# Splitting half of the last store into 112 + 8 + 8 rows, so that eight DMA engines carry 9 row halves and eight carry 7

## Chip, cores, metric

One core of a Trainium2 chip. The metric is the device time of one execution in microseconds; all runs quoted are at full clock. The kernel before took 781.05 us (three runs, 780.86 to 781.10).

## The reference

```python
# logits (32, 128, 4, 4096) f32, prior (32, 128, 4) f32
prior_probs = softmax(prior, axis=-1)
mixture = np.sum(prior_probs[..., None] * softmax(logits, axis=-1), axis=2)   # (32, 128, 4096)
```

For each of 4096 rows, four softmaxes over 4096 columns are mixed with four weights: 268 MB are read and 67 MB written, with little arithmetic for each byte.

## The kernel before

A tile is 128 rows, one on each partition; there are 32 tiles (`U = 32`). ScalarE takes the exponentials with their sums, VectorE weighs and adds, and two sets of buffers alternate. Loads are issued by SyncE and most stores by ScalarE. The very last tile is finished and stored in two column halves, which is what the change touches:

```python
def store(u, acc, eng, lo=0, hi=V):
    st = eng.dma_start(out=ov[u // J, u % J, :, lo:hi], in_=acc[:, lo:hi])
    stores[u] = only(st, adds[u, H - 1])        # waits for the last add alone
# ... (cut)
for k in range(g, h + 1):
    n = 2 if u == U - 1 and k == H - 1 else 1   # last tile, last head: two column halves
    w = V // n
    for c in range(n):
        add(k, mul, c * w, (c + 1) * w)
        if n > 1:
            store(u, acc, nc.sync, c * w, (c + 1) * w)
```

The softmax here doesn't subtract the row's maximum and nothing guards it: scores larger than these inputs give would overflow.

## Time and profile before

| | before |
|---|---|
| time, us (median of the first 3 runs) | 781.05 |
| span of the profiled execution, us | 779.3 |
| busy: VectorE, ScalarE, DMA | 67%, 60%, 99.9% |
| first half of the last store issued, us | 771.19 |
| VectorE done, us | 773.42 |
| last landing, us | 778.37 |
| first half's issue to last landing ("the tail"), us | 7.18 |

The first rows say that the DMA engines are the bound; the others lay out the end, the only place that the change can reach. The timeline of SyncE's issues at the end has two pieces, whose columns are start, duration, engine, line, operation and tiles:

```profile
771.19 0.33 SPq L113 DMA_DIRECT2D out_dram<-ltile  x1
773.45 0.33 SPq L113 DMA_DIRECT2D out_dram<-ltile  x1
```

The reader is to see that the second half is issued 0.03 us after VectorE ends and that nothing more is issued afterwards; the other 5 us are the DMA engines emptying their queues.

### The profile page before, as it was taken

The page shows a single profiled execution, that of the slowest core. Times are in us where ns is not written, and L with a number is a line of the kernel's source. Part 1 is how long each engine was busy: PE and PEld are TensorE (multiplying, and loading weights), DVE is VectorE, ACT ScalarE, POOL GpSimd, SP SyncE. Part 2 cuts the span into 40 slices and gives each one's busy share as a digit, 9 for nine tenths or more (in the row PEclk, how much of TensorE's full clock was granted, in tenths as well). Part 3 has the DMA queues.
Part 4 walks back from the last instruction along what each step waited for, and adds up shares of the span by engine and source line. Part 5 has one row for each costly group of instructions (what it writes and reads, how often), then busy time and mean ns, then how long its engine had stood idle before and what let it go on. Part 6 is the DMA issues. An engine that isn't in the chain of part 4 may idle for free.

```text
span 779.3 us, 654 instructions
## 1 busy us (share of the span) xinstructions
DVE 521.0 (67%) x174; ACT 466.7 (60%) x258; POOL 8.3 (1%) x41
## 2 busy tenths in 40 slices
DVE  4447875558755587555775557855578655689886
ACT  4476555775457755577555675546765567657782
POOL 0000000000000000000000000000000000000000
DMA  9999999999999999999999999999999999999998
GB/s 407 457 417 401 470 407 434 428 461 428 405 467 403 458 420 433 442 443 418 431 454 407 454 408 467 420 415 447 432 442 417 463 399 463 410 427 433 434 429 377
DMA packets 10117, 335.66 MB, mean 431 GB/s; under 512 B 1136, under 2 KB 1136, under 8 KB 1152
## 3 DMA queue, kind: packets, MB, share of 16 engines
q1 hardware_dynamic: 6048, 276.83, 82.3%
q10 hardware_dynamic: 4064, 58.79, 17.6%
q14 instruction: 5, 0.04, 0.0%
HBM read 268.50 MB, written 67.11 MB: 431 GB/s over the span
## 4 chain that ended last, share of the span: by engine, by line
DMA 64%; ACT 27%; DVE 6%; issue 2%; POOL 0%; DVEq 0%; POOLq 0%
DMA ltile<-in_logits_dram 62%; ACT ebuf L159 19%; ACT ltile L159 8%; DVE obuf L177 5%; DMA out_dram<-obuf 2%; DVE ltile L183 1%; POOL coeff L170 0%; DVE rden L168 0%; DVEq L240 0%; POOLq L240 0%; POOLq L170 0%
## 5 line engine op out<-in xcount | busy, mean ns | idle before, releaser
L183 DVE SCALAR_TENSOR_TENSOR obuf<-ebuf,coeff,obuf 128x4096 f32<-128x4096 f32 x90 | 403.6, 4484 | 3.8 <-POOL coeff L170 0.6
L159 ACT ACTIVATE ebuf<-ltile 128x4096 f32<-128x4096 f32 x90 | 322.9, 3589 | 7.4 <-DMA ltile<-in_logits_dram 7.4
L159 ACT ACTIVATE ltile<-ltile 128x4096 f32<-128x4096 f32 x38 | 137.3, 3614 | 280.6 <-DMA ltile<-in_logits_dram 280.6
L168 DVE RECIPROCAL rden<-dsum 128x4 f32<-128x4 f32 (+1 forms) x36 | 6.3, 175 | 227.9 <-ACT ebuf L159 225.1
L177 DVE TENSOR_SCALAR obuf<-ltile,coeff 128x4096 f32<-128x4096 f32 x30 | 70.6, 2353 | 10.2 <-POOL coeff L170 10.2
L183 DVE SCALAR_TENSOR_TENSOR ltile<-ltile,coeff 128x4096 f32<-128x4096 f32 (+1 forms) x7 | 27.0, 3875 | 0.8 <-POOL coeff L170 0.6
L159 ACT ACTIVATION_READ_ACCUMULATOR ebuf<-ltile 128x1 f32 x90 | 16.8, 186 | 0.0
L170 POOL TENSOR_TENSOR coeff<-rden,pp 128x4 f32<-128x4 f32 (+1 forms) x36 | 7.2, 200 | 755.3 <-DVE rden L168 745.4
L159 ACT ACTIVATION_READ_ACCUMULATOR ltile<-ltile 128x1 f32 x38 | 7.1, 186 | 0.0
L139 DVE TENSOR_REDUCE pmax<-pr 16x256 f32<-16x1024 f32 x1 | 1.2, 1208 | 7.8 <-DMA pr<-in_prior_dram 7.8
L141 ACT ACTIVATE pr<-pr 16x1024 f32<-16x1024 f32 x1 | 1.1, 1055 | 7.8 <-DVE pr L140 7.8
L177 DVE TENSOR_SCALAR ltile<-ltile,coeff 128x4096 f32<-128x4096 f32 x2 | 4.7, 2354 | 0.6 <-POOL coeff L170 0.6
L144 DVE TENSOR_TENSOR pn<-pr,pmax 16x1024 f32<-16x1024 f32 x1 | 1.9, 1939 | 0.1
L141 ACT ACT_TABLE_LOAD x1 | 1.3, 1283 | 1.2 <-PEq L229 1.2
L142 DVE TENSOR_REDUCE pmax<-pr 16x256 f32<-16x1024 f32 x1 | 1.2, 1207 | 1.1 <-ACT pr L141 1.1
L149 DVE STREAM_TRANSPOSE pp<-pn 32x256 f32<-32x256 f32 x4 | 1.7, 435 | 0.1
L143 DVE RECIPROCAL pmax<-pmax 16x256 f32<-16x256 f32 x1 | 1.7, 1741 | 0.0
L140 DVE TENSOR_TENSOR pr<-pr,pmax 16x1024 f32<-16x1024 f32 x1 | 1.2, 1211 | 0.0
L138 POOL MEMSET pn<- 32x1024 f32 x1 | 0.9, 941 | 0.3 <-POOLq L229 0.3
L229 POOL MEMSET const-bfloat16-1.0<- 128x1 bf16 x1 | 0.1, 106 | 0.0
L229 POOL MEMSET const-uint8-127<- 128x1 uint8 x1 | 0.1, 106 | 0.0
L229 POOL MEMSET const-float32-0.0<- 128x1 f32 x1 | 0.1, 103 | 0.2 <-issue 0.2
(1 smaller groups left out, 0.1 us busy)
## 6 DMA issues: line engine op xcount, KB each, us to landing
out_dram<-obuf ACTq DMA_DIRECT2D x28, 2048.0 KB, 29.4
ltile<-in_logits_dram SPq DMA_DIRECT2D x7, 4096.0 KB, 26.1
ltile<-in_logits_dram SPq DMA_DIRECT2D x2, 2048.0 KB, 30.9
out_dram<-obuf SPq DMA_DIRECT2D x2, 2048.0 KB, 33.9
out_dram<-ltile SPq DMA_DIRECT2D x1, 2048.0 KB, 17.2
out_dram<-ltile SPq DMA_DIRECT2D x2, 1024.0 KB, 4.8
ltile<-in_logits_dram SPq DMA_DIRECT2D x28, 30.9
pr<-in_prior_dram ACTq DMA_DIRECT2D x1, 64.0 KB, 7.0
```

Of the source, the lines that this page charges most:

```text
L139: nc.vector.reduce_max(pmax, pr, axis=AX.X)
L140: nc.vector.tensor_sub(pr, pr, pmax.unsqueeze(2).to_broadcast([G, R, H]))
L141: nc.scalar.activation(pr, pr, AF.Exp)
L142: nc.vector.reduce_sum(pmax, pr, axis=AX.X)
L143: nc.vector.reciprocal(pmax, pmax)
L144: nc.vector.tensor_mul(pn[0:G].rearrange("g h r -> g r h"), pr, pmax.unsqueeze(2).to_broadcast([G, R, H]))
L149: nc.vector.transpose(pp[32 * t : 32 * (t + 1)], pq[:, :, :, 32 * t : 32 * (t + 1)])
L159: ex = nc.scalar.activation(es[h], lt[:, h], AF.Exp, accum_out=dsum[:, u, h : h + 1])
L168: rc = nc.vector.reciprocal(rden[:, u, h : h + n], dsum[:, u, h : h + n])
L170: mul = nc.gpsimd.tensor_mul(coeff[:, u, h : h + n], rden[:, u, h : h + n], ppu[:, h : h + n])
L177: st = nc.vector.tensor_scalar(out=acc[:, lo:hi], in0=es[h][:, lo:hi], scalar1=coeff[:, u, h : h + 1], scalar2=None, op0=ALU.mult,)
L183: st = nc.vector.scalar_tensor_tensor(out=acc[:, lo:hi], in0=es[h][:, lo:hi], scalar=coeff[:, u, h : h + 1], in1=acc[:, lo:hi], op0=ALU.mu ...
```

## The change

The intent is to level the ragged end: some DMA engines finish later than others, so the first eight engines get 9 row halves in the first half store and the other eight get 7, in place of 8 each.

```diff
-    def store(u, acc, eng, lo=0, hi=V):
-        st = eng.dma_start(out=ov[u // J, u % J, :, lo:hi], in_=acc[:, lo:hi])
-        stores[u] = only(st, adds[u, H - 1])
+    def store(u, acc, eng, lo=0, hi=V, rows=((0, P),)):
+        for a, b in rows:
+            st = eng.dma_start(out=ov[u // J, u % J, a:b, lo:hi], in_=acc[a:b, lo:hi])
+            stores[u] = only(st, adds[u, H - 1])
@@ in the loop over the column halves
-                            store(u, acc, nc.sync, c * w, (c + 1) * w)
+                            rows = ((0, 112), (112, 120), (120, P)) if c == 0 else ((0, P),)
+                            store(u, acc, nc.sync, c * w, (c + 1) * w, rows)
```

## The prediction

> **What bounds the kernel now.** I read the page first, then the chain of waits, then the last few microseconds in short stretches, then the single packet and landing records of the trace. The page:
>
> ```profile
> DVE 521.0 (67%) x174; ACT 466.7 (60%) x258; POOL 8.3 (1%) x41
> ...
> DMA  9999999999999999999999999999999999999998
> ...
> q1 hardware_dynamic: 6048, 276.83, 82.3%
> q10 hardware_dynamic: 4064, 58.79, 17.6%
> q14 instruction: 5, 0.04, 0.0%
> ...
> HBM read 268.50 MB, written 67.11 MB: 431 GB/s over the span
> ```
>
> The reader should see that no compute engine is over 67%, while the 16 DMA engines are busy in every slice: 82.3 + 17.6 = 99.9% of 16 engines' span. The kernel moves 335.6 MB, and that is its time. No byte is removed by the change, so all but the last few microseconds of the 779.3 us span stay as they are. Queue 14 has five small instruction fetches; they matter below.
>
> How does it end? The two half stores of the last tile are the last work. The page's issue line, the waits of the DMA queue of SyncE in the last 16 us, and the stretches of the end:
>
> ```profile
> out_dram<-ltile SPq DMA_DIRECT2D x2, 1024.0 KB, 4.8
> ```
> ```profile
> SPq L113 <- DVE ltile L183: 16.3, 2, 14.4
> SPq L240 <- DMA out_dram<-ltile: 4.4, 2, 2.4
> ```
> ```profile
> 770.00:772.00 2.00, 2.00 (x2) 0.00 (x0) 0.00 (x0) 1.00 0.96 410
> 772.00:774.00 2.00, 1.42 (x1) 0.00 (x0) 0.00 (x0) 1.00 1.00 410
> 774.00:776.00 2.00, 0.00 (x0) 0.00 (x0) 0.00 (x0) 1.00 1.01 422
> 776.00:777.00 1.00, 0.00 (x0) 0.00 (x0) 0.00 (x0) 1.00 0.96 401
> 777.00:777.25 0.25, 0.00 (x0) 0.00 (x0) 0.00 (x0) 1.00 0.33 131
> 777.25:777.50 0.25, 0.00 (x0) 0.00 (x0) 0.00 (x0) 1.00 0.24 98
> 777.50:777.75 0.25, 0.00 (x0) 0.00 (x0) 0.00 (x0) 1.00 0.16 66
> 777.75:778.00 0.25, 0.00 (x0) 0.00 (x0) 0.00 (x0) 1.00 0.00 0
> ```
>
> The last two columns are the DMA share and GB/s; a packet counts where it starts. Up to 777.00 all engines run, although VectorE finished at 773.42 (764.29 + 9.13 in the timeline): the stores stand in line behind earlier traffic. The chain of waits printed in the profile ends at VectorE's drain, but that is the inference losing the DMA; SyncE's final wait ends with the store's landing. After 777.00 comes a ragged end: (0.33 + 0.24 + 0.16) x 0.25 us x 16 = 2.9 us of engine time, nine packets of 0.309 us. Some engines are simply later than others. That raggedness is what the change is aimed at.
>
> The packet records say by how much. Each half store is 128 packets of 8 KB, 8 for each engine, 0.309 us each (26.5 GB/s). The completion packets after the very last one start at 777.05 to 777.16 (ten engines), 777.23, 777.32, 777.48, 777.74, 777.87 and 778.01; the landing follows 0.36 us later (the last at 778.37). The mean is 777.29, so perfect balance would save 778.01 - 777.29 = 0.72 us, 0.09%. That is the ceiling of any change of this kind.
>
> Why three stragglers? The 16 landings of a whole-tile load at 136 us spread over 0.44 us. After the fetch at 147.9 us one landing trails by 0.75 us, after that at 194.0 us another by 1.18; the one at 704.7 us adds a third at 0.64. The late places persist because no engine ever idles to catch up.
>
> **What the Trainium skill says.** "DMA: Bandwidth & Descriptors", section "Why a DMA increments its semaphore by 16 and not by 1": a transfer runs on the largest k up to 16 that divides its slowest dimension, the lowest-numbered k of the core's engines. So 112 rows use 16 engines with 7 rows each, and 8 rows use engines 0 to 7 with one row each. The trace agrees for 16 (the prior load of 16 rows left 16 packets of 4 KB); it has no case of 8 and doesn't number the engines.
>
> "SBUF - State Buffer", section "Door 1: The DMA port swizzle": DMA bandwidth depends on how many of 16 ports the partitions reach; partitions 112 to 115 share one port, likewise 116 to 119, 120 to 123 and 124 to 127. The same DMA page, "The descriptor swizzle", has each engine of a 128-partition transfer on one port of its own. The trace has one sign that crowding costs: the prior load writes 16 rows into partitions 0 to 15, four ports by that table. Its packets take 0.159 us, but the 32 KB packets behind them take 1.55 us on all engines (one 1.67) where others take 1.213: 0.34 us too much. The first store, also a switch of queue, has 2.418 us packets behind it as everywhere, so switching isn't the cost. It could still be that queue's first use.
>
> "Runtime: NRT & Kernel Launch", section "Instruction fetch mechanics": the sequencer fetches its own instructions through its own DMA queue. The trace agrees: the five queue 14 packets of 8 KB, at 147.9, 194.0, 511.1, 704.7 and 774.8 us, and the stragglers of above.
>
> **The change part by part.** Removed: one issue of 128 half rows. Added: one of 112 and two of 8. Bytes, arithmetic and the second half's issue are the same.
>
> *Issue.* The first half is issued at 771.19 for 0.333 us, the second at 773.45, when its VectorE piece ends. Two more issues with their semaphore waits take about 2 x 0.38 = 0.76 us and end near 772.3, before 773.45. First packets come 0.83 us after issue (772.02); the 8-row transfers are ready near 772.4 and 772.8, before the 7 rows are through (772.02 + 7 x 0.31 = 774.2). Cost 0. The second half's first packets are ready near 774.28, so a fast engine with 7 rows may idle under 0.1 us; it isn't last.
>
> *Balance.* If the three stragglers have numbers 8 to 15, each loses one packet: the last completion goes from 778.01 to 777.70. The first eight gain one: from 777.05-777.48 to 777.36-777.79. The end becomes 777.70 to 777.79: -0.22 to -0.31 us. If one of the last two stragglers is in the first eight it ends at 777.87 or 778.01 plus 0.31: +0.17 to +0.31 us.
>
> *Ports.* The last 16 rows are read by engines 0 to 7, four at once from one port. The prior load's excess was 0.34 us for 4 KB rows; estimate for 8 KB: 0.68 us, twice, 1.35 us for the first eight. They have 777.70 - 777.5 = about 0.2 us to spare, so the end would move by about +0.8 to +1.1 us against before. Seven rows for each engine no longer match groups of four partitions either; I allow 0 to 0.5 us for that (estimate: up to a fifth of 7 x 0.309).
>
> *End.* SyncE waits for the semaphores two at a time in fixed order; before, the store's was in the second last pair, with one 0.06 us step behind it. Two more transfers shift the numbering: 0 to +0.06 us.
>
> **Rivals.**
> 1. Balance alone works: about 780.8 us. For it: the stragglers are real and steady, and the first load's engines start as a group of seven at 1.02-1.07 us and nine at 1.16-1.58 us, which looks like a first and a second eight, the second later. Against: fetches, not start order, made the stragglers.
> 2. The stragglers are among the first eight: 781.05 + 0.3 = 781.35. I can't exclude it, for the records carry no engine number; whoever chose the first eight presumably had a reason.
> 3. Port crowding eats the gain: 781.9 to 782.6. For it: the 0.34 us behind the prior load, equal on all engines. Against: that was writing, and a lone case.
> 4. An additional fetch from the longer instruction stream falls on a straggler: +0.3 us. The one at 774.8 fell on an engine that ended at 777.13, so I give it little.
>
> **Range and chances.** I give rival 1 about 0.35, rivals 2 and 4 together 0.2, rival 3 0.45. The middle of that mixture is about 781.3, slightly slower than 781.05 and my choice; 780.6 to 782.6 spans from the full gain with a little noise (the three runs spread 0.24 us) to port crowding in both the small transfers and the seven-row one. 2% is 15.6 us, while all of the last store lasts under 6 us: within 2% is close to sure.
>
> **What would show it.** Queue 1 has more packets: 16 + 8 + 8 completion packets for the first half in place of 16. If 8 KB packets near 774.2-775 stay at 0.31 us, ports don't matter; if the 8-row ones, or those behind them, take 0.6 to 1.2 us, rival 3 holds. If the ragged end narrows and the last landing comes near 778.1, rival 1 holds; if one engine ends near 778.3 with 17 even packets of 0.309 us, rival 2. The prediction is wrong if anything before 771 us moves, or if the small transfers start late enough to hold up the second half.

## The result, and the profile after

The changed kernel took 782.74 us (median of 6, 782.36 to 783.16) against 781.11 (median of 6, 780.86 to 781.13). The ratio is 1.0021, 95% interval 1.0008 to 1.0034. Ratios are the mean time of one kernel's fast runs over that of the other's in the same rounds, so not quite the ratio of the medians. So the change costs 1.6 us, a fifth of a per cent: "same" at 2%, and just above the predicted range (780.6 to 782.6).

In the profile the tail grew from 7.18 to 9.14 us (771.02 to 780.17), by 1.96 us; that it began 0.17 us earlier hides a part. These are the stretches of the end (stretch, its length, three engines, clock, DMA share, GB/s); those of before stand in the prediction:

```profile
770.00:772.00 2.00, 2.00 (x2) 0.00 (x0) 0.00 (x0) 1.00 1.00 418
772.00:774.00 2.00, 1.26 (x1) 0.00 (x0) 0.00 (x0) 1.00 1.00 336
774.00:776.00 2.00, 0.00 (x0) 0.00 (x0) 0.00 (x0) 1.00 0.94 279
776.00:778.00 2.00, 0.00 (x0) 0.00 (x0) 0.00 (x0) 1.00 0.89 348
778.00:780.00 2.00, 0.00 (x0) 0.00 (x0) 0.00 (x0) 1.00 0.18 74
```

This is the line to learn from. Between 772 and 776 the engines are as busy as before (0.94 to 1.00), but they move 336 and 279 GB/s where they moved 410 and 422. Busy here means "a packet is under way", and the packets had become slow. An 8 KB packet took 0.309 us before; in the changed kernel 46 of the 256 took over 0.4 us (3 of 256 before), and the slowest five, starting at 774.6 to 775.0, when the 8-row transfers run, 1.10, 1.17, 1.35, 1.41 and 1.52 us. The time beyond 0.309 us of all these packets together, the excess, is 18.1 us, or 1.13 us for each of 16 engines, against 0.10 before.

The page's queue and issue lines, and SyncE's waits of the last 19 us:

```profile
q1 hardware_dynamic: 6064, 276.83, 82.2%
q10 hardware_dynamic: 4064, 58.79, 17.6%
q14 instruction: 5, 0.04, 0.0%
```
```profile
out_dram<-ltile SPq DMA_DIRECT2D x1, 1024.0 KB, 6.9
out_dram<-ltile SPq DMA_DIRECT2D x1, 896.0 KB, 4.8
```
```profile
SPq L114 <- DVE ltile L184: 15.1, 2, 14.4
SPq L244 <- DMA out_dram<-ltile: 6.0, 1, 6.0
```

The bytes are those of before and the packets 16 more (6064 to 6048): the completion packets of two transfers on eight engines each, as predicted. The second half, issued as early as before (773.29, VectorE had ended at 773.26), needs 6.9 us to land in place of 4.9 (773.45 to 778.37), and SyncE's last wait for it is 6.0 us long.

### The profile page after: what moved, and what is told of

Its sections match the earlier page's. It is cut to its first block, busy times and chain, and to the rows that moved or that the text cites. A ratio compares the mean times of both kernels' runs of the same rounds, so it can differ in the third digit from the quotient of the medians.

```text
span 781.1 us, 656 instructions
## 1 busy us (share of the span) xinstructions
DVE 521.0 (67%) x174; ACT 466.9 (60%) x258; POOL 8.4 (1%) x41
## 3 DMA queue, kind: packets, MB, share of 16 engines
q1 hardware_dynamic: 6064, 276.83, 82.2%
## 4 chain that ended last, share of the span: by engine, by line
DMA 64%; ACT 27%; DVE 6%; issue 2%; POOL 0%; DVEq 0%; POOLq 0%
DMA ltile<-in_logits_dram 62%; ACT ebuf L160 19%; ACT ltile L160 8%; DVE obuf L178 5%; DMA out_dram<-obuf 2%; DVE ltile L184 1%; POOL coeff L171 0%; DVE rden L169 0%; DVEq L244 0%; POOLq L244 0%; POOLq L171 0%
```

## The experiments

The theory after the result: SBUF's side is crowded. Rows 112 to 119 lie on two ports, four on each, by the port table of the Trainium skill ("SBUF - State Buffer", section "Door 1: The DMA port swizzle"), so four engines would read from one port at once; the 112-row transfer may be crowded too. Rivals: small transfers or additional issues cost this much wherever they read; or the stragglers sit among the first eight engines, which were given more.

"Scratch" runs leave the kernel before as it is and add a store from the finished half tile into an internal scratch tensor, so that load is added and nothing taken away. All ten kernels gave the correct result.

On noise: the 95% intervals of these ratios reach 1.0 to 1.3 us to either side (spread rows below: 0.9995 to 1.0022), so a difference under 1 us rests on two other things: whether the ranges of the runs lie apart, and the tail, which comes from one profiled execution of each kernel.

**Issues alone.**

```diff
-   store(u, acc, nc.sync, c * w, (c + 1) * w)
+   cuts = (0, 1792, 1920, 2048) if c == 0 else (2048, 4096)
+   for lo, hi in zip(cuts, cuts[1:]):
+       store(u, acc, nc.sync, lo, hi)
```

> The first half of the last store goes as three transfers of all 128 rows, 1792, 128 and 128 columns wide: the byte split 7:1:1... of the changed kernel, but on all engines and each engine on its own port. Port theory (crowding of rows 112 to 127 on four ports made the loss): 781.1 to 781.4 us, for two more issues cost nothing. Rival (two more issues, completions and small packets in the tail cost the 1.6 us): 782.4 or more.

Measured 781.12 us against 781.00; tail 7.24 us, +0.06. Three issues in place of one, with the same split of bytes (14:1:1 in columns as in rows, not the 7:1:1 of the expectation), cost next to nothing. Additional issues are out; transfers of few rows are tested next.

**Two additional 8-row stores, spread and crowded.** The rows 0, 4, .., 28 lie on eight different ports, the rows 112 to 119 on two.

```diff
+   if c == 0:   # spread: rows 0:32:4 and 1:32:4; crowded: rows 112:120 and 120:128
+       only(nc.sync.dma_start(out=scratch[0:8, 0:2048], in_=acc[0:32:4, 0:2048]), adds[u, k])
+       only(nc.sync.dma_start(out=scratch[8:16, 0:2048], in_=acc[1:32:4, 0:2048]), adds[u, k])
```

> The kernel before, with two additional 8-row half stores (two more 8 KB packets for each of the first eight engines, 0.62 us each) into a scratch tensor, from rows 0,4,..,28 and 1,5,..,29, which lie on eight different ports. Port theory: packets stay near 0.31 us; the end is 781.1 to 781.3 us if the stragglers are engines 8 to 15, and 781.7 if the last one is among the first eight. Rival (8-row transfers are slow by themselves, wherever they read): 782.5 or more.

> The same two additional 8-row half stores into scratch, but read from rows 112 to 119 and 120 to 127, four rows on one port. Port theory: each takes about 1.2 us in place of 0.31 on the first eight engines, 2.4 us in all, so they end near 779.6 to 780 and the time is 782.4 to 783.2 us. Rival (8-row transfers as such, or imbalance): the same time as with the spread rows.

Spread 781.62 us (+0.62 against 781.00), crowded 783.55 (+2.55), with equal bytes and transfers; in the edit only the partitions differ. The ranges lie apart (781.54 to 781.87 and 783.48 to 783.63), and the crowded time is above its expected 782.4 to 783.2. The tails are 7.81 and 9.78 us, so four rows on a port cost 1.97 us for two such transfers. The stretches, first of the spread run, then of the crowded one:

```profile
774.00:776.00 2.00, 0.00 (x0) 0.00 (x0) 0.00 (x0) 1.00 0.88 361
776.00:778.00 2.00, 0.00 (x0) 0.00 (x0) 0.00 (x0) 1.00 0.80 328
```
```profile
774.00:776.00 2.00, 0.00 (x0) 0.00 (x0) 0.00 (x0) 1.00 1.06 266
776.00:778.00 2.00, 0.00 (x0) 0.00 (x0) 0.00 (x0) 1.00 0.75 242
```

In each stretch compare GB/s with the share. Spread: 361 at 0.88, 328 at 0.80, both 410 GB/s for a fully busy set of engines, the usual rate. Crowded: 266 at 1.06 and 242 at 0.75, so 251 and 323. The packets themselves are slow; the slowest took 2.11 us.

The spread run also answers the second rival. Its last completion packets start at 777.31 to 777.40 on eight engines, at 777.85 to 777.90 on five, and at 778.27, 778.34 and 778.62 on three. An engine with two more packets can't be among the early eight: the earliest of before ended at 777.05, and 0.62 us later is 777.67. So the early eight are those without an additional packet. The stragglers of before, at 777.74 or later, aren't among them; so all three are among the eight engines that an 8-row transfer uses, and the last of them ends 0.62 us (two packets) later than before. In that run the second half was also issued late (773.80), which left a doubt: the next pair of runs.

**One additional store, and four-row stores.**

```diff
+   if c == 0:   # once: rows 0:32:4 alone; four rows: 0:16:4 and 1:16:4
+       only(nc.sync.dma_start(out=scratch[0:8, 0:2048], in_=acc[0:32:4, 0:2048]), adds[u, k])
```

> The kernel before with one additional 8-row half store into scratch from rows 0, 4, .., 28 (eight different ports). If the last straggler is one of the first eight engines, one more packet moves the end by 0.31 us: 781.3 to 781.4 us, and two gave 0.62. If the 0.62 us of the run with two came from the later issue of the second half, 781.0 to 781.1 us here, for one more issue ends before that half is ready.

> The kernel before with two additional 4-row half stores into scratch, rows 0, 4, 8, 12 and 1, 5, 9, 13: two more packets for each of the first four engines only. If the last straggler is among engines 0 to 3: 781.6 us, as with the 8-row ones. If among 4 to 7: 781.0 to 781.1 us, and only the second or third straggler or none moves in the landings.

One store: 781.13 us against 781.02, nearer to the second expectation, with overlapping ranges (781.07 to 781.17 and 780.88 to 781.13). The time alone doesn't settle it. The profile speaks for the first: the tail is 7.48 us, +0.30, and it began 0.17 us earlier than in before's profile. A measure that doesn't depend on the start is the time from the last landing of the whole-tile store ahead (the latest engine's) to the last landing of all: before 773.53 to 778.37, 4.84 us; with one additional packet 773.35 to 778.50, 5.15; with two 773.51 to 778.98, 5.47. That is 0.31 us for each packet, with the second half issued on time (773.28) in the run with one. Its packets stay fast too (2 of 264 over 0.4 us), so spread rows don't owe their speed to a late second half. Four-row stores: 781.62 us (+0.60), 773.57 to 779.03, 5.46 us: the latest straggler is even among the four engines that a 4-row transfer uses. If the late engines keep their order, the second latest behaves likewise: from its landing in the store ahead to its last packet it takes 4.49 us before (773.38 to 777.87) and 5.11 in this run (773.39 to 778.51); the third apparently isn't.

**112 rows and one transfer of 16.**

```diff
-   rows = ((0, 112), (112, 120), (120, P)) if c == 0 else ((0, P),)
+   rows = ((0, 112), (112, P)) if c == 0 else ((0, P),)
```

> First half as 112 rows and one transfer of 16 rows on all engines: 8 packets for each engine, no imbalance, and the same four crowded ports. Port theory: 4 rows on a port at a time, about +0.9 us, and something for the 112 rows: 782.0 to 783.2 us. Rival (the loss came from two packets too many on late engines among the first eight): 781.1 us.

Measured 782.17 us against 781.00, tail 8.34 us: +1.17 and +1.16. Every engine should have its 8 packets here, so 1.2 us of loss come without any imbalance. The packets are slow instead, by 1.10 us of excess for each engine, and the rate shows it:

```profile
774.00:776.00 2.00, 0.00 (x0) 0.00 (x0) 0.00 (x0) 1.00 0.97 287
```

**Every other row.**

```diff
-   rows = ((0, 112), (112, 120), (120, P)) if c == 0 else ((0, P),)
+   rows = ((0, 112), (112, P, 2), (113, P, 2)) if c == 0 else ((0, P),)   # used as slices
```

> The changed kernel, but the two 8-row transfers take rows 112, 114, .., 126 and 113, 115, .., 127: two rows on a port at a time instead of four, same bytes, same engines. Port theory: the two transfers lose about 0.3 us each in place of about 0.9, so the time falls from 782.7 to 781.7 to 782.3 us. Rival (the rows 112 to 127 or the 9-to-7 split as such make the loss): 782.7 us still.

Measured 781.75 us against 781.00; the changed kernel had 782.74 against 781.11. Taking two rows from a port instead of four, with the same bytes and rows, cuts the loss from 1.63 to 0.75 us; 0.9 us come back, and the excess falls from 18.1 to 12.0 us, 0.75 us for each of the eight engines. (The profiled executions differ more, tails of 9.14 and 7.70 us.) One thing besides differs: SyncE took 0.78 and 1.37 us to issue the two strided transfers, so the second half went out only at 774.18, 0.86 us after VectorE had ended. That leaves engines idle (12 to 15 packets under way near 775), but it may also thin the traffic beside the small transfers; this run doesn't part the two effects. The stretch of this run beside the changed kernel's 279 GB/s at 0.94:

```profile
774.00:776.00 2.00, 0.00 (x0) 0.00 (x0) 0.00 (x0) 1.00 0.93 340
```

**Two transfers of 64 rows.**

```diff
-   rows = ((0, 112), (112, 120), (120, P)) if c == 0 else ((0, P),)
+   rows = ((0, 64), (64, P)) if c == 0 else ((0, P),)
```

> First half as rows 0 to 63 and rows 64 to 127, both on 16 engines with 4 packets each. Port theory: each reaches only eight ports, two engines on each, so 4 x 2 x 0.309 = 2.47 us a transfer in place of 1.24, 4.9 in all: +1.5 to +2.6 us, 782.6 to 783.7 us. Rival (only transfers of few rows, or rows 112 to 127 alone, are slow; or engines are chosen by partition so that ports stay apart): 781.1 to 781.3 us.

Measured 783.48 us against 781.00, +2.5, the full dose that the port count gives. The stretches while the first half goes out:

```profile
772.00:774.00 2.00, 1.27 (x1) 0.00 (x0) 0.00 (x0) 1.00 0.98 221
774.00:776.00 2.00, 0.00 (x0) 0.00 (x0) 0.00 (x0) 1.00 1.01 254
```

All engines are busy and move 221 GB/s, close to half of before's 410 in the same stretch: eight ports for sixteen engines. So neither few rows nor the rows 112 to 127 are needed for the effect. Two transfers of every other row, 64 rows on all 16 ports, would have been the counter-test; they weren't run.

**The 112-row form by itself, with its control.**

```diff
+   if c == 0:   # control: scratch[0:128, 0:1792] from acc[0:128, 0:1792], the same bytes
+       only(nc.sync.dma_start(out=scratch[0:112, 0:2048], in_=acc[0:112, 0:2048]), adds[u, k])
```

> The kernel before with one additional store of rows 0 to 111 of the first half into scratch: 7 packets more for each engine, 7 x 0.309 = 2.16 us without crowding, so 783.2 us. If seven rows for each engine break the match of engines and ports, 783.4 to 784.2 us, and the packets of this transfer average over 0.35 us.

> Its control: an additional store of the same bytes as 128 rows of 1792 columns into scratch, each engine on its own port: 8 x 0.27 = 2.16 us more, 783.2 us under both theories. The difference between the two runs is the cost of the 112-row form itself.

783.53 and 782.92 us (both against 781.00): 0.61 us for the form, 0.44 us by the tails (9.76 and 9.32). The control came out below its expected 783.2; its tail is longer by 2.14 us, as expected, but began 0.25 us earlier than before's. In the stretch from 774, first 112 rows, then the control:

```profile
774.00:776.00 2.00, 0.00 (x0) 0.00 (x0) 0.00 (x0) 1.00 1.05 356
```
```profile
774.00:776.00 2.00, 0.00 (x0) 0.00 (x0) 0.00 (x0) 1.00 1.01 414
```

That the engines fall out of step with the ports with 112 rows is my reading; how the 112 rows are dealt to engines no record shows.

No run beat the kernel before. Relief for the stragglers would have to load the other eight engines, and every transfer of 4 or 8 rows here went to the stragglers' eight.

## Why the prediction was wrong

- **The bound, the place and the class** were right: nothing changed ahead of the tail but its usual wandering, and the time moved by 0.2%. (The last store lasts 7.18 us from its first issue to its last landing, not "under 6 us"; nothing hangs on it.)
- **Issue: cost 0.** Right for the end (+0.06 us for three issues). An engine with 7 rows was to idle under 0.1 us; from 774.6 to 775.0 only 12 to 14 packets are under way on 16 engines, probably because the second half's issue took 0.69 us in place of 0.33. That those engines aren't the last ones is inferred.
- **Balance.** I put my stronger belief on the stragglers being engines 8 to 15 (-0.22 to -0.31 us) and reasoned that whoever chose the first eight had a reason. All three are in the eight that got more: +0.31 us for each packet. A reason that one supposes isn't evidence; rival 2 needed a run.
- **Ports.** The mechanism, rival 3, was right. Whether the 1.55 us packets behind the prior load, from which I took it, were crowding too, no run tested. The size of 0.68 us for an 8-row transfer is neither borne out nor refuted: the crowded minus the spread run gives 1.97 / 2 = 0.99 us, but in the changed kernel itself two rows on a port in place of four save 0.9 / 2 = 0.45 us.
- **The step that failed** is "They have 777.70 - 777.5 = about 0.2 us to spare, so the end would move by about +0.8 to +1.1 us": it assumed stragglers outside the first eight. They are inside, so nothing is to spare, the added packet counts in full, and rivals 2 and 3, which I had weighed as alternatives, add up. By my own terms 0.31 + 1.35 + (0 to 0.5) = 1.66 to 2.16 us, 782.7 to 783.2 us. By the measured ones: 0.31 for the packet, 0.44 to 0.61 for the 112-row form, and 0.9 for the crowding of the two 8-row transfers, as far as halving the crowd took it away. They sum to 1.7 to 1.8 us for the 1.63 timed and 1.96 in the profile. The sum isn't exact: the run with every other row lost 0.75 us, which packet and form alone would make (0.75 to 0.92), and with the 1.97 us of the scratch pair in place of 0.9 it would be 2.7 to 2.9. That the crowding costs time is shown; its share of the 1.63 us is an estimate.
- **The middle, 781.3 us,** came from giving 0.35 to the full gain; with the engines' places known it would not have had any of that. (781.3 is about the median of the mixture; its mean is 781.6.)
- **Fetches, rival 4.** There are five in all twelve profiles, so no additional one came. The last began at 775.8 us in the changed kernel and at 774.8 before; whether it fell on the last engine no record shows.
- **End: 0 to +0.06 us.** From the last landing to the end of the span it was 0.91 us before and 0.95 after: right.

What stays open: how the loss divides between the crowding and the rest, which engines in number the stragglers are, whether each instruction fetch always falls on the same engine (the first two fetches, near 147.8 and 193.8 us, are followed by one and two late landings in all twelve profiles, trailing by 0.65 to 0.88 and by 1.05 to 1.19 us), and why the tail's start wanders.

## What to carry to other kernels

Keep a store that ends a DMA-bound kernel in the form in which all 16 engines read from different partition groups; a few rows cut off the end of a tile sit on few ports and move at a fraction of the rate (221 to 279 GB/s here in place of 410 to 422) while every engine still shows as busy, so read GB/s beside the busy share. Before giving some DMA engines more work, find out which are late: an additional spread-out transfer into scratch that loads only the engines in question tells it in one run. And when two rivals don't exclude one another, add them before setting the range.

## What the Trainium skill lacked or had wrong

- "DMA: Bandwidth & Descriptors", section "Rules for kernel authors", says of two transfers to disjoint partition halves that they serialize because both use the same 16 engines. That understates it: for two stores of 64 rows these runs show 221 GB/s in place of 410, and 2.5 us more for 1 MB that otherwise takes 8 x 0.309 = 2.5 us, so twice the time. The reason, 8 ports for 64 rows, stands in "SBUF - State Buffer", section "Door 1: The DMA port swizzle", but not beside that rule.
- The same section of "SBUF - State Buffer" has the port table and rates of whole transfers by the ports reached, which these runs bear out. It lacks what one packet takes when engines crowd on a port amid other traffic: the slowest five of 8 KB took 1.10 to 1.52 us in the changed kernel, the slowest 2.11 us in the crowded run, against 0.309 us before.
- "DMA: Bandwidth & Descriptors", section "The descriptor swizzle", gives the rows of each engine for 128 partitions only. 112 rows cost 0.44 to 0.61 us more than the same bytes over 128 rows.
- "Runtime: NRT & Kernel Launch", section "Instruction fetch mechanics", calls the cost of a fetch mostly hidden. What it cost the instruction stream no run tested; for the DMA engines, the first fetch (a packet of 0.31 us) is followed by one landing that trails from then on: 0.44 us of spread before it, 0.75 us after it, 1.18 us after the second. The end of the kernel waits for such late engines.
- No page has the issue time of small strided transfers: SyncE took 0.75 and 0.96 us for 8 rows four partitions apart, 0.38 and 0.29 us for 8 adjacent rows, 0.33 us for 128 rows in the kernel before.
